# An fp32 two-layer hybrid trunk on one core: issuing the odd mixer's small steps by an estimate of the engines

## The chip, the core and the metric

The kernel runs on one core of one Trainium2 chip. Its engines are TensorE (PE; PEld is its weight load), VectorE (DVE), ScalarE (ACT), GpSimd (POOL) and SyncE (SP), which issues most DMAs. The metric is the device time of one launch in microseconds (us); lower is better. Times come from repeated runs; the profile is of one further execution.

## The reference

Sixteen meta tokens are put ahead of 256 frames of width 1024, T = 272 columns in all. Two layers follow, each `h += 1/2 SwiGLU(RMSNorm h); h += Mixer(RMSNorm h); h += 1/2 SwiGLU(RMSNorm h)`, in fp32, with a feed-forward width of 2816. The even mixer has a top-k sparse attention beside a chunkwise retention. The odd mixer, which the change is mostly about, is cut here to what matters:

```
cq, ck, cv, dx = split_cols(h @ w_in, [512, 128, 128, 512])
cq, ck = rms_norm(cq per head, c_qn), rms_norm(ck per head, c_kn)   # 8 query heads, 2 key heads of 64
yc = swa_sinks(cq, ck, cv, sinks)        # softmax over a window, the meta keys and one sink per head
yd = pool_mixer(dx, d_mix, d_scale)      # (mean over the last 2, 4, 8, 16 rows - x) @ mix, per group of 128
y  = concat(yc, yd) @ w_out              # 1024 x 1024
```

## The kernel before

**Layout.** The state h lies transposed, as eight tiles of 128 features x 272 columns. An fp32 product is made of three fast matmuls: operand and weight are each split into a rounded part (hi) and its remainder (lo), and `mmw` issues whi x xhi (L256), whi x xlo (L257), wlo x xhi (L258). One call is a block: one 128x128 weight tile against 256 or 272 columns. There are 2616 blocks in a fixed order, given by the `order_*` functions, and the weights lie packed in that order. Eight blocks make a unit (512 KB).

**Weights.** The class `Weights` loads chunks of one or two units over SP's queue into three buffers (`load`), and splits each unit: ACT rounds it to whi (L165), DVE subtracts to wlo (L166; POOL for a few units). Splits run four units ahead of PE; a ring holds six. In the mixers a unit is split in two halves, one at its first block and one in the middle (`halves`). At the start, h comes in four loads and the first weights in parts of 256 KB and whole units; the first 32 blocks go in rounds of one, one, two and four k over four groups (`order_ffn_in0`).

**The order of the small steps.** Everything but blocks is a generator (a task). Each block ends in `tick`, which moves a clock by one and resumes the tasks that are due; a task says by a number in the table `W` in how many ticks (blocks) it wants to go on. All engines take their instructions in this program order, so a step issued too early makes its engine wait with everything behind it. `drain` ticks until no task is left. `norm_r` (ones-matmul L311, table load, Ln, Exp, three DVE products) is issued at fixed blocks.

**The odd mixer** (`odd`). Ten groups of eight blocks (k = 0 to 7): keys, four pairs of query heads (256 columns), values, four pool groups; queries and pool groups alternate at the end. The first two groups leave out k = 7 until both are there (`_late_last_k`). A finished group is scaled by r into SBUF (`evac`, L435). Then `head_norm` (square on ACT L442, ones-matmul L446, `rsqrt` with Ln, Exp, one DVE product and POOL's L275 to L277, scale L450), `to_tokens` (transposes of the values, L459), or `pool_mix` (POOL sums L853, DVE L857, matmul L860, ACT L863, DVE L865). `attend` handles a pair of heads: scores L482, maxima on DVE L491, exponentials on ACT L498, normalisation L505, transposes ("turn", three PSUM banks) L513, copies L517 to L519, product with the values L528, outputs L530 and L532. One such attention is started every 8 ticks. The output has eight row tiles m of eight k: k = 7 to 4 (pools) and then k = 0 to 3 (attention) for the first four m, then the other four; `finish` adds a row tile to h, makes the next layer's xhi (L285) and xlo (L286), and POOL sums squares. PSUM has eight banks, one per accumulating group or small result.

Of the kernel before, what the change touches and what calls it, by code (L numbers as in the profile page):

```python
# [18 lines left out]
T = 272  # L19
# [40 lines left out]
def order_ffn_in0():  # L60

    g = [(p, j) for j in range(KF) for p in range(2)]
    return ([(x, k) for r in (range(1), range(1, 2), range(2, 4), range(4, 8)) for x in g[:4] for k in r]
            + [(x, k) for x in g[4:] for k in range(KD)])


def order_ffn_out():
# [7 lines left out]
OD_GROUPS = ([("ck", 0), ("cq", 0), ("cv", 0), ("cq", 1), ("dx", 3), ("cq", 2), ("dx", 2), ("cq", 3)]  # L75
             + [("dx", i) for i in (1, 0)])
# [16 lines left out]
def order_od_out():  # L93
    a, b = range(4), range(4, 8)
    return ([(m, k) for m in a for k in (7, 6, 5, 4)] + [(m, k) for m in a for k in range(4)]
            + [(m, k) for m in b for k in (4, 5, 6, 7, 0, 1, 2, 3)])
# [8 lines left out]
N_UNITS = sum(len(ORDERS[p[0]]()) for p in PHASES) // UNIT  # L105


def chunk_units():

    sizes, left = [1, 1, 1, 1], N_UNITS - 4  # L110
    while left:
        n = min(2, left)
        sizes.append(n)
        left -= n
    return sizes
# [3 lines left out]
W = dict(first_sq=2, hid=6, hid_lo=1, hn_sum=15, hn_out=15, od_hn=(4, 10), tok=15, tok_out=1,  # L119
         ev=dict(max=1, max2=2, exp=3, exp2=2, norm=2, norm2=2, turn=4, copy=2, pv=4, lo=1), ev_every=22,  # L120
         od=dict(max=1, max2=2, exp=2, exp2=2, norm=1, norm2=1, turn=3, copy=1, pv=3, lo=1), od_every=8,
         ix=10, ix_relu=1, ix_add=2, top_a=5, top_b=3, meta_k=8, meta=4, rope=10, rope_done=24, ret_every=10, ret_mask=1, ret_v=1, ret_s=2,
         ret_sum=7, ret_out=14, ret_lo=2, pool=3, pool_g=3, pool_mm=3, pool_lo=2)


class Weights:


    RAW, RING, AHEAD = 3, 6, 4

    def __init__(self, nc, pool, w):
        self.nc, self.pool, self.w = nc, pool, w
# [4 lines left out]
        self.halves, self.todo = False, None  # L137
        self.loaded = self.split_to = self.i = 0
# [12 lines left out]
    def load_part(self, i):  # L151

        n = UNIT * 128
        if i == 0:
            self.raw[0] = self.pool.tile([128, 2 * n], F32, tag="raw", name="raw", bufs=self.RAW)
        o = i * n // 2
        self.nc.sync.dma_start(self.raw[0][:, o:o + n // 2], bass.AP(
            tensor=self.w.tensor, offset=self.w.offset + o, ap=[[n, 128], [1, n // 2]]))
        self.loaded = 1

    def part(self, u, s):
# [4 lines left out]
        eng.tensor_tensor(lo[:, s], src[:, s], hi[:, s].bitcast(F32), op=OP.subtract)  # L166

    def split(self, upto, halves=False):
        while self.split_to < min(upto, N_UNITS):
            u, n = self.split_to, UNIT * 128  # L170
            c = self.chunk_of[u]
            self.load(c + 1)
            o = (u - self.first[c]) * n
            self.src[u] = self.raw[c][:, o:o + n]
            hi = self.pool.tile([128, n], F32R, tag="whi", name="whi", bufs=self.RING)
            lo = self.pool.tile([128, n], F32R, tag="wlo", name="wlo", bufs=self.RING)
            self.parts[u] = (hi, lo)
            self.parts.pop(u - self.RING, None)
            self.part(u, slice(0, n // 2) if halves else slice(0, n))
            if halves:  # L180
                self.todo = u
            self.split_to += 1
            if not halves:
                self.done_with(u)

    def second_half(self):
        if self.todo is not None:
            self.part(self.todo, slice(UNIT * 64, UNIT * 128))
            self.done_with(self.todo)
            self.todo = None  # L190
# [20 lines left out]
class Trunk:  # L211
    def __init__(self, tc, ctx, a, out):
        self.tc, self.nc, self.a, self.out = tc, tc.nc, a, out
# [4 lines left out]
        self.w = Weights(self.nc, self.ring, a["w"])  # L218
# [4 lines left out]
    def spawn(self, gen):  # L223
        self.tasks.append([self.clock, gen])

    def run_tasks(self):
        for t in list(self.tasks):
            while t[1] is not None and t[0] <= self.clock:
                try:
                    t[0] = self.clock + max(1, next(t[1]) or 1)  # L230
# [4 lines left out]
    def tick(self):  # L235
        self.clock += 1
        self.run_tasks()
# [12 lines left out]
    def bank(self, tag):  # L250
        return self.psum.tile([128, 512], F32, tag="bank", name=tag, bufs=8)

    def mmw(self, ps, hi, lo, start, stop):
        mm = self.nc.tensor.matmul
        wh, wl = self.w.next()
        mm(ps, wh, hi, start=start, stop=False)  # L256
        mm(ps, wh, lo, start=False, stop=False)  # L257
        mm(ps, wl, hi, start=False, stop=stop)  # L258
        self.tick()

    def rsqrt(self, out, mean, on=None):

# [6 lines left out]
        nc.scalar.activation(r0, r0, AF.Exp, scale=-0.5)  # L269
        nc.vector.scalar_tensor_tensor(u, mean, EPS, r0, op0=OP.add, op1=OP.mult)  # L270
# [8 lines left out]
    def prep_x(self, m, norm, c):  # L279

        nc = self.nc
        g = self.par[:, norm * KD + m:norm * KD + m + 1]
        hi = self.keep.tile([128, T], F32R, tag="xhi", name="xhi", bufs=KD)
        lo = self.keep.tile([128, T], F32R, tag="xlo", name="xlo", bufs=KD)
        nc.scalar.activation(hi[:, c], self.h[m][:, c], AF.Copy, scale=g)  # L285
        nc.vector.scalar_tensor_tensor(lo[:, c], self.h[m][:, c], g, hi[:, c].bitcast(F32),  # L286
                                       op0=OP.mult, op1=OP.subtract)
        self.x[m] = (hi, lo)

    def finish(self, m, ps, coef, norm, c):  # L290
# [11 lines left out]
        else:  # L302
            sq = self.keep.tile([128, T], F32, tag="sq", name="sq", bufs=2)
            nc.gpsimd.tensor_tensor(sq[:, c], h, h, op=OP.mult)  # L304
            nc.gpsimd.tensor_tensor(self.acc[:, c], self.acc[:, c], sq[:, c], op=OP.add)

    def norm_r(self, c):
# [7 lines left out]
        self.r = r  # L315


    def start(self):
        nc, a, keep = self.nc, self.a, self.keep
        hall = keep.tile([128, NPAR + KD * T], F32, name="h")  # L320
        self.par = hall[:, :NPAR]
# [13 lines left out]
        self.w.load_part(0)  # L335
        load_h(1, 2)
        self.w.load_part(1)
        load_h(2, 4)
        self.w.load(2)
        load_h(4, 8)  # L340
        self.w.load(Weights.RAW)
# [13 lines left out]
        self.x, self.acc, self.r = {}, None, None  # L355

    def first_x(self):

        nc, c = self.nc, slice(0, T)
        for m in range(KD):  # L360
            self.prep_x(m, 0, c)
            if m == 0:
                self.w.split(1, halves=True)
            elif m == 1:
                self.w.second_half()
            elif m == 3:
                self.w.split(2)

        def squares():
            yield W["first_sq"]  # L370
            for m in range(KD):
                sq = self.keep.tile([128, T], F32, tag="acc" if m == 0 else "sq", name="sq", bufs=2)
                nc.scalar.activation(sq, self.h[m], AF.Square)
                if m == 0:
                    self.acc = sq
                else:
                    nc.gpsimd.tensor_tensor(self.acc, self.acc, sq, op=OP.add)
                yield W["first_sq"]
        self.spawn(squares())

    def ffn(self, c, next_norm, first=False):
        nc = self.nc
        self.w.halves = False
        with ExitStack() as es:
# [3 lines left out]
            self.r = None  # L388
# [23 lines left out]
            for (p, j), k in (order_ffn_in0 if first else order_ffn_in)():  # L412
                if (p, j) not in banks:
                    banks[p, j] = self.bank("mm")[:, :n]
                hi, lo = self.x[k]
                d = done[p, j] = done.get((p, j), 0) + 1
                self.mmw(banks[p, j], hi[:, c], lo[:, c], d == 1, d == KD)
                if p == 1 and d == KD:
                    if j == (2 if first else 0):
                        self.norm_r(c)  # L420
                    self.spawn(act(j, banks.pop((0, j)), banks.pop((1, j))))
            for m, k in order_ffn_out():
# [10 lines left out]
    def evac(self, ps, pool, tag, bufs, c=slice(0, T)):  # L433
        t = pool.tile([128, T], F32, tag=tag, name=tag, bufs=bufs)
        self.nc.vector.tensor_tensor(t[:, c], ps, self.r[:, c], op=OP.mult)  # L435
        return t

    def head_norm(self, raw, gain, pool, put, c=slice(0, T), wt=None):

        nc = self.nc  # L440
        sq = pool.tile([128, T], F32, tag="hn_sq", name="hn_sq", bufs=2)[:, c]
        nc.scalar.activation(sq, raw[:, c], AF.Square)  # L442
        wt = wt or (W["hn_sum"], W["hn_out"])
        yield wt[0]
# [3 lines left out]
        self.rsqrt(rr, ps, nc.gpsimd)  # L448
        yield wt[1]
# [3 lines left out]
    def to_tokens(self, raw, put):  # L453

        nc = self.nc
        yield W["tok"]
# [3 lines left out]
        yield W["tok_out"]  # L460
        put(ps)

    def attend(self, pool, st, wt, i, qT, kT, v_cols, bias, yhi, ylo, sinks=None):
# [8 lines left out]
        e = int(sinks is not None)  # L472
        so = (0, NKEYS[0] + e)
# [560 lines left out]
```

## Time and profile before

| | us |
|---|---|
| median of the runs | 1092.91 (1092.13 to 1094.56) |
| the profiled execution | 1095.3 |
| its span, first to last instruction | 1093.5 |
| PE busy in it | 1077.0 |
| DVE busy | 713.5 |
| ACT busy | 521.1 |
| POOL busy | 178.9 |

A program shows what each engine did in the span. A busy PE is modelled from pipelined matmuls, whose durations overlap; the rate at which blocks start says more. "Idle before" a row is the time its engine stood still ahead of it, and the name behind the arrow is what ended that.

### The profile page before, as it was taken

What the parts mean: (1) busy time and instruction counts of PE and PEld (TensorE: products, weight loads), DVE (VectorE), ACT (ScalarE), POOL (GpSimd) and SP (SyncE); (2) the same over time, 40 slices, a digit from 0 to 9 for tenths busy, and PEclk for the clock granted to TensorE, in tenths of its full rate; (3) what the DMA queues carried; (4) which work ended last, traced back from release to release, by engine and by line L of the source; (5) the groups of instructions that cost most, each with busy time, mean ns of one, the idle gap of its engine ahead of it and who ended that gap; (6) DMA issues with size and microseconds to landing.
All of it is one profiled execution on the core that took longest, in us unless ns stands there. A gap on an engine that the chain in (4) does not pass through costs nothing.

```text
span 1093.5 us, 20686 instructions
## 1 busy us (share of the span) xinstructions
PE 1077.0 (98%) x8601; PEld 1056.8 (97%) x8601; DVE 713.5 (65%) x1217; ACT 521.1 (48%) x861; POOL 178.9 (16%) x223
## 2 busy tenths in 40 slices
PE   8999999999999999999999999999998899999998
PEld 7999999999899999999999999999997699999998
DVE  4776655399885677766655576665558767777642
ACT  6554443456545645544434454443436436554431
POOL 2000001448431741000002100000224221000000
PEclk9999999999999999999999999999999899999999
DMA  6554444543563334544554455454443224655551
GB/s 244 201 215 173 175 154 171 184 150 131 187 208 116 117 126 184 201 185 170 177 188 159 154 193 186 161 192 175 174 171 117 78 103 171 216 205 177 182 201 39
DMA packets 29805, 183.54 MB, mean 168 GB/s; under 512 B 3904, under 2 KB 6336, under 8 KB 8592
## 3 DMA queue, kind: packets, MB, share of 16 engines
q1 hardware_dynamic: 29440, 181.29, 45.9%
q8 instruction: 67, 1.10, 0.4%
q0 software_dynamic: 272, 0.94, 0.3%
q14 instruction: 26, 0.21, 0.1%
HBM read 180.02 MB, written 1.05 MB: 166 GB/s over the span
## 4 chain that ended last, share of the span: by engine, by line
PE 92%; DVE 3%; ACT 2%; DMA 1%; SPq 1%; issue 1%; POOL 0%; DVEq 0%; ACTq 0%
PE mm L256 29%; PE mm L257 29%; PE mm L258 29%; DMA raw<-in_w 1%; DVE wlo L166 1%; PE sd L513 1%; PE sd L528 1%; ACT whi L165 1%; PE sd L482 1%; PE sd L446 0%; SPq L630 0%; PE sd L703 0%; PE sd L729 0%; PE sd L737 0%; PE sd L599 0%
## 5 line engine op out<-in xcount | busy, mean ns | idle before, releaser
L256 PE MATMUL mm<-xhi,whi 128*128 128x272 f32 (+1 forms) x1816 | 532.8, 293 | 1.4 <-ACT whi L165 1.4
L258 PE MATMUL mm<-xhi,wlo 128*128 128x272 f32 (+1 forms) x1816 | 522.3, 288 | 1.0 <-DVE wlo L166 1.0
L257 PE MATMUL mm<-xlo,whi 128*128 128x272 f32 (+1 forms) x1816 | 521.9, 287 | 0.2
L166 DVE TENSOR_TENSOR wlo<-raw,whi 128x1024 fp32r<-128x1024 f32 (+1 forms) x394 | 414.9, 1088 | 81.0 <-ACT whi L165 80.0
L165 ACT ACTIVATE whi<-raw 128x1024 fp32r<-128x1024 f32 (+1 forms) x407 | 346.3, 895 | 30.5 <-PE mm L257 25.0
L256 PEld LDWEIGHTS mm<-xhi,whi 128*128 128x128 f32 x1816 | 344.0, 189 | 8.1 <-issue 4.5
L258 PEld LDWEIGHTS mm<-xhi,wlo 128*128 128x128 f32 x1816 | 344.5, 190 | 1.5 <-DVE wlo L166 1.5
L257 PEld LDWEIGHTS mm<-xlo,whi 128*128 128x128 f32 x1816 | 343.5, 189 | 1.5 <-DVE xlo L286 0.6
L258 PE MATMUL mm<-hhi,wlo 128*128 128x272 f32 (+1 forms) x704 | 201.4, 286 | 0.0
L257 PE MATMUL mm<-hlo,whi 128*128 128x272 f32 (+1 forms) x704 | 201.4, 286 | 0.0
L256 PE MATMUL mm<-hhi,whi 128*128 128x272 f32 (+1 forms) x704 | 201.1, 286 | 0.0
L256 PEld LDWEIGHTS mm<-hhi,whi 128*128 128x128 f32 x704 | 132.6, 188 | 0.0
L257 PEld LDWEIGHTS mm<-hlo,whi 128*128 128x128 f32 x704 | 132.5, 188 | 0.0
L258 PEld LDWEIGHTS mm<-hhi,wlo 128*128 128x128 f32 x704 | 132.5, 188 | 0.0
L399 ACT ACTIVATE gr<-gr 128x272 f32<-128x272 f32 (+1 forms) x88 | 37.7, 428 | 153.8 <-DVE gr L397 153.8
L285 ACT ACTIVATE xhi<-h 128x272 fp32r<-128x272 f32 (+1 forms) x48 | 24.6, 520 | 154.3 <-DVE h L294 150.7
L294 DVE SCALAR_TENSOR_TENSOR h<-mm,h 128x272 f32<-128x272 f32 (+1 forms) x48 | 20.8, 433 | 115.7 <-PE mm L258 115.7
L404 ACT ACTIVATE hhi<-ur 128x272 fp32r<-128x272 f32 (+1 forms) x88 | 37.6, 428 | 91.0 <-DVE ur L401 91.0
L301 POOL TENSOR_TENSOR acc<-h 128x272 f32<-128x272 f32 (+1 forms) x5 | 3.2, 634 | 431.5 <-DVE h L294 431.5
L398 DVE TENSOR_TENSOR ur<-mm,r 128x272 f32<-128x272 f32 (+1 forms) x88 | 38.2, 434 | 43.9 <-PE mm L258 43.8
L407 DVE TENSOR_TENSOR hlo<-ur,hhi 128x272 fp32r<-128x272 f32 (+1 forms) x88 | 38.5, 438 | 41.9 <-ACT hhi L404 41.9
L304 POOL TENSOR_TENSOR sq<-h 128x272 f32<-128x272 f32 (+1 forms) x35 | 22.2, 634 | 157.8 <-DVE h L294 157.8
(161 smaller groups left out, 867.0 us busy)
## 6 DMA issues: line engine op xcount, KB each, us to landing
raw<-in_w SPq DMA_DIRECT2D x165, 1024.0 KB, 4.8
tab<-in_tab SPq DMA_DIRECT2D x8, 272.0 KB, 5.0
raw<-in_w SPq DMA_DIRECT2D x4, 512.0 KB, 6.2
sw<-ev_t SPq DMA_DIRECT2D x32, 34.0 KB, 3.3
out<-h SPq DMA_DIRECT2D x8, 128.0 KB, 1.7
h<-in_h SPq DMA_DIRECT2D x1, 544.0 KB, 7.3
raw<-in_w SPq DMA_DIRECT2D x2, 256.0 KB, 3.5
h<-in_h SPq DMA_DIRECT2D x1, 272.0 KB, 5.7
```

Source lines behind the costliest of these rows:

```text
L165: self.nc.scalar.activation(hi[:, s], src[:, s], AF.Copy)
L166: eng.tensor_tensor(lo[:, s], src[:, s], hi[:, s].bitcast(F32), op=OP.subtract)
L256: mm(ps, wh, hi, start=start, stop=False)
L257: mm(ps, wh, lo, start=False, stop=False)
L258: mm(ps, wl, hi, start=False, stop=stop)
L285: nc.scalar.activation(hi[:, c], self.h[m][:, c], AF.Copy, scale=g)
L294: nc.vector.scalar_tensor_tensor(h, ps, coef, h, op0=OP.mult, op1=OP.add)
L304: nc.gpsimd.tensor_tensor(sq[:, c], h, h, op=OP.mult)
L398: nc.vector.tensor_tensor(ur[:, c], pu, r, op=OP.mult)
L399: nc.scalar.activation(gr[:, c], gr[:, c], AF.Silu)
L404: nc.scalar.activation(hi[:, c], ur[:, c], AF.Copy)
L407: nc.vector.tensor_tensor(lo[:, c], ur[:, c], hi[:, c].bitcast(F32), op=OP.subtract)
```

## The change

- The start: h is loaded tile by tile, the weights of the first 32 blocks four blocks at a time beside it, and those blocks run k by k over four groups. All chunks have two units.
- `_late_last_k` holds back the last two k of the first two groups in place of the last one.
- A class `Plan` keeps an estimate of when each engine is free and each tensor ready, fed by wrappers around the engines. In the odd mixer a task waits, in place of a number of ticks, for `after(engine, operands)`: until the operands are estimated ready at that engine's time or PE's. `room(k)` makes it wait until k of the eight banks are free beside a reserve. Evacuations are tasks too. A wlo subtraction is held until its whi is estimated ready, or its unit is wanted.
- The odd mixer's groups go keys, first queries, values, the other queries, then the pool groups. At most two attentions are in flight. The sinks are copied by POOL. The head norms' rsqrt ends on DVE. The output runs k = 7 to 4 over all eight m, two m to a bank, then k = 0 to 3 by m; `finish2` handles two row tiles together, with the squares on ACT, and its last ones run on into the next layer.
- From 110 blocks before the odd mixer the splits run further ahead, by up to eight halves; after the even mixer the ring has ten units.
- `norm_soon` issues a norm when its sum is estimated ready. The three pauses of the even mixer's meta attention are 8 ticks in place of 4.

The core of the diff:

```diff
-    out = [(g, k) for g in groups[:late] for k in range(kn - 1)]
-    out += [(g, kn - 1) for g in groups[:late]]
+    out = [(g, k) for g in groups[:late] for k in range(kn - 2)]
+    out += [(g, k) for k in (kn - 2, kn - 1) for g in groups[:late]]
...
+    return [(x, k) for k in range(KD) for x in g[:4]] + [(x, k) for x in g[4:] for k in range(KD)]
...
-OD_GROUPS = ([("ck", 0), ("cq", 0), ("cv", 0), ("cq", 1), ("dx", 3), ("cq", 2), ("dx", 2), ("cq", 3)]
-             + [("dx", i) for i in (1, 0)])
+OD_GROUPS = ([("ck", 0), ("cq", 0), ("cv", 0), ("cq", 1), ("cq", 2), ("cq", 3)] + [("dx", i) for i in (3, 2, 1, 0)])
...
+    return ([(m, k) for k in (7, 6, 5, 4) for m in range(KD)] + [(m, k) for m in range(KD) for k in range(4)])
...
+MORE_AHEAD = ([OD_AT + b for b in (-110, -8, 16, 108, 112, 144)], (0, 8, 8, 3, 3, 0))
...
+    def ready(self, eng, aps, slack=0.0):
+        t = max((self.at.get(a.name, 0.0) for a in aps), default=0.0)
+        return t <= max(self.free["PE"], self.free[eng]) + slack
...
+                busy, mode = (0.5 if half else 1.0) * 1.67 * n, self.HALF if half else self.FULL
+            if mode != self.mode:
+                busy, self.mode = busy + 200, mode
+            late = 150
+        elif eng == "DVE":
+            busy, late = 95 + 1.03 * n, 120
+            if op == "tensor_tensor_reduce":
+                busy += 80
+            if self.free["POOL"] > self.free["DVE"]:
+                busy *= 1.25
+        elif eng == "ACT":
+            busy, late = 100 + 0.84 * n, 150
...
+    def low(self, upto=None):
+
+        while self.lows and (self.plan.ready("DVE", [self.lows[0][2]]) if upto is None and self.wait
+                             else upto is None or self.lows[0][0] <= upto):
...
-        if j == 0:
-            self.split(u + self.AHEAD, self.halves)
-        elif j == UNIT // 2:
-            self.second_half()
+        if j in (0, UNIT // 2):
+            extra = int(np.interp(self.i, *MORE_AHEAD))
+            self.split(2 * (u + self.AHEAD) + extra - (self.halves and j == 0))
+        self.low(u)
...
+    def room(self, k):
+
+        while self.live + k + self.reserve > 8:
+            yield 1
...
+        nc.vector.tensor_tensor(h, two(ps), h, op=OP.add)
+        yield self.after("ACT", h)
+        for m in ms:
+            self.x_hi(m, norm, c)
+        sq = [self.keep.tile([128, T], F32, tag="sq", name="sq", bufs=2) for _ in ms]
+        for m in ms:
+            nc.scalar.activation(sq[m - ms[0]][:, c], self.h[m][:, c], AF.Square)
+        yield self.after("DVE", self.xh[ms[1]])
+        for m in ms:
+            self.x_lo(m, norm, c)
...
+    def norm_soon(self, c):
+
+        self.r = None
+        while self.summed < KD:
+            yield 1
+        yield self.after("PE", self.acc)
+        self.norm_r(c)
...
+        self.w.load_part(0, 2)
+        self.w.load_part(2, 2)
+        for m in range(1, KD):
+            load_h(m, m + 1)
+            self.w.load_part(4 * m, 4)
+        for i in (32, 40):
+            self.w.load_part(i, 8)
...
+            yield self.after("ACT", ps)
+            yield from self.rsqrt_steps(rr, ps)
+            self.live -= 1
+            yield self.after("DVE", rr)
...
-                    while i not in got["cq"] or not got["ck"] or not st["vC"]:
+                    while i not in got["cq"] or not got["ck"] or not st["vC"] or st.get("turned", 0) < i - 1:
...
+            self.live, self.reserve, self.w.wait = 0, 2, True
+            self.spawn(self.norm_soon(c))
+            self.spawn(attention())
...
+                    if g == OD_GROUPS[-1]:
+                        self.reserve = 4
...
+                self.mmw(banks[b][:, half * SEQ:half * SEQ + SEQ], hi[:, cx], lo[:, cx], d == 1, d > 14, True)
+                if d == 16:
+                    self.spawn(self.finish2(b, banks.pop(b), next_norm))
+                    self.run_tasks()
```

## Rows read from the trace of the kernel before

**Rows 1.** The page's busy times of the engines over the span.
```profile
PE 1077.0 (98%) x8601; PEld 1056.8 (97%) x8601; DVE 713.5 (65%) x1217; ACT 521.1 (48%) x861; POOL 178.9 (16%) x223
```

**Rows 2.** Busy time by stretch: stretch, length, engines (instructions), granted clock, DMA share, GB/s.
```profile
30.00:100.00 70.00, 70.00 (x558) 70.00 (x556) 52.43 (x84) 37.00 (x55) 0.00 (x0) 1.00 0.53 194
...
760.00:819.00 59.00, 59.00 (x474) 59.00 (x473) 30.71 (x39) 22.85 (x29) 12.10 (x16) 1.00 0.49 183
819.00:845.00 26.00, 22.05 (x169) 20.21 (x169) 19.95 (x52) 14.23 (x36) 10.47 (x13) 1.00 0.37 131
845.00:885.00 40.00, 35.70 (x274) 30.98 (x273) 25.34 (x76) 18.91 (x53) 9.00 (x12) 0.87 0.16 55
...
960.00:1025.00 65.00, 65.00 (x549) 65.00 (x548) 45.42 (x71) 32.49 (x48) 0.00 (x0) 1.00 0.53 193
```

**Rows 3.** PE's waits: line, what it waited for, us in total, times, longest.
```profile
PE sd L446 <- ACT hn_sq L442: 3.4, 2, 1.8
PE sd L513 <- DVE at_s L505: 2.5, 3, 1.9
...
PE mm L256 <- ACT oyhi L863: 1.1, 2, 0.6
PE sd L648 <- DVE ms L645: 1.0, 1, 1.0
...
PE sd L860 <- DVE at_m L502: 0.8, 1, 0.8
```

**Rows 4.** PE's timeline at the start: first matmuls of blocks 5, 11, 16, 33.
```profile
7.00 0.39 PE L256 MATMUL mm<-xhi,whi 128*128 128x272 f32 x1
...
12.53 0.36 PE L256 MATMUL mm<-xhi,whi 128*128 128x272 f32 x1
...
15.87 0.36 PE L256 MATMUL mm<-xhi,whi 128*128 128x272 f32 x1
...
22.36 0.29 PE L256 MATMUL mm<-xhi,whi 128*128 128x272 f32 x1
```

**Rows 5.** DMA from 0 to 40 us: GB/s per us; one load, KB, us to landing.
```profile
GB/s 0 35 319 201 209 293 317 385 423 418 406 250 74 176 401 393 221 401 442 393 401 229 41 8 25 8 115 344 418 311 385 426 98 66 287 410 303 0 0 0
...
h<-in_h SPq DMA_DIRECT2D x1, 168.0 KB, 2.3
```

**Rows 6.** PE's timeline: first block of the odd mixer, first of the last layer.
```profile
814.38 0.29 PE L256 MATMUL mm<-xhi,whi 128*128 128x272 f32 x1
...
900.62 0.28 PE L256 MATMUL mm<-xhi,whi 128*128 128x256 f32 x1
```

**Rows 7.** The chain that ended last, pieces in the odd mixer: start, us, what.
```profile
842.87 0.43 PE sd L446 x2
843.67 1.09 PE sd L513 x10
...
846.66 1.25 PE sd L528 x20
...
851.94 0.90 PE sd L482 x8
```

**Rows 8.** Timelines of POOL and DVE: end of a head norm's rsqrt; a DVE product.
```profile
826.26 1.32 POOL L275 TENSOR_TENSOR rs<-rs,rs 128x272 f32<-128x272 f32 x1 [8.37 <-DVE rs L270]
...
828.17 1.09 POOL L277 TENSOR_TENSOR hn_r<-rs,rs 128x272 f32<-128x272 f32 x1
...
822.01 0.44 DVE L272 SCALAR_TENSOR_TENSOR rs<-rs,rs 128x272 f32<-128x272 f32 x1
```

**Rows 9.** Timelines of PE and ACT: a small matmul and its reader.
```profile
833.13 0.70 PE L446 MATMUL sd<-hn_sq,ones_h 128*128 128x256 f32 x2 [1.76 <-ACT hn_sq L442]
...
833.93 0.48 ACT L268 ACTIVATE rs<-sd,eps 128x256 f32<-128x256 f32 x1 [0.33 <-PE sd L446]
```

**Rows 10.** PE's timeline at the start of the last layer.
```profile
902.88 0.38 PE L256 MATMUL mm<-xhi,whi 128*128 128x256 f32 x1
903.40 0.39 PE L257 MATMUL mm<-xlo,whi 128*128 128x256 f32 x1
```

More of the change, by code (lines that the diff above doesn't have):

```diff
@@ new lines, with __init__, __getattr__, call @@
+class Engine:
+    def __init__(self, real, plan, name):
+        self.real, self.plan, self.name = real, plan, name
+    def __getattr__(self, op):
+        f = getattr(self.real, op)
+        def call(*a, **k):
+            r = f(*a, **k)
+            self.plan.note(self.name, op, a, k)
+            return r
+        return call
+class Engines:
+    def __init__(self, nc, plan):
+        self.nc, self.sync = nc, nc.sync
+        self.tensor, self.vector, self.scalar, self.gpsimd = (
+            Engine(e, plan, n) for e, n in ((nc.tensor, "PE"), (nc.vector, "DVE"), (nc.scalar, "ACT"),
+                                            (nc.gpsimd, "POOL")))
+    def get_next_instruction_name(self):
+        return self.nc.get_next_instruction_name()
@@ L165, in part @@
         self.nc.scalar.activation(hi[:, s], src[:, s], AF.Copy)
[L166 to L183, printed above, removed]
-                self.done_with(u)
@@ new lines, in lengthen, with open_unit @@
+    def lengthen(self, pool):
+        self.pool2 = pool
+    def open_unit(self, u):
+        n = UNIT * 128
+        c = self.chunk_of[u]
+        self.load(c + 1)
+        o = (u - self.first[c]) * n
+        self.src[u] = self.raw[c][:, o:o + n]
+        pool, name, bufs = self.pool, "", self.RING
+        if self.pool2:
+            if self.at >= self.RING:
+                pool, name, bufs = self.pool2, "2", self.MORE
+            self.at = (self.at + 1) % (self.RING + self.MORE)
+        self.parts[u] = tuple(pool.tile([128, n], F32R, tag=t + name, name=t + name, bufs=bufs) for t in ("whi", "wlo"))
+        self.parts.pop(u - self.RING - self.MORE, None)
@@ L192, in done_with, with split @@
+    def split(self, goal):
+        while self.split_to < min(goal, 2 * N_UNITS):
+            u, half = divmod(self.split_to, 2)
+            if not half:
+                self.open_unit(u)
+            n = min(2 - half, goal - self.split_to)
+            self.split_to += n
+            self.pending[u] = self.pending.get(u, 2 if not half and n == 1 else 1)
+            self.part(u, slice(half * UNIT * 64, (half + n) * UNIT * 64))
     def done_with(self, u):
@@ L223, in spawn, with after @@
     def spawn(self, gen):
-        self.tasks.append([self.clock, gen])
+        self.tasks.append([self.clock, gen, None])
+    def after(self, eng, *aps):
+        return lambda: self.plan.ready(eng, aps)
+    def room(self, k):
+        while self.live + k + self.reserve > 8:
+            yield 1
     def run_tasks(self):
+        if self.w.wait:
+            self.w.low()
         for t in list(self.tasks):
-            while t[1] is not None and t[0] <= self.clock:
+            while t[1] is not None and t[0] <= self.clock and (t[2] is None or t[2]()):
                 try:
-                    t[0] = self.clock + max(1, next(t[1]) or 1)
+                    v = next(t[1])
+                    t[2] = v if callable(v) else None
+                    if t[2] is None:
+                        t[0] = self.clock + max(1, v or 1)
                 except StopIteration:
@@ L233, in run_tasks, with tick @@
                     self.tasks.remove(t)
-    def tick(self):
+    def tick(self, idle=True):
         self.clock += 1
+        if idle:
+            self.plan.free["PE"] += 125
         self.run_tasks()
@@ L250, in bank, with mmw, rsqrt_steps @@
     def bank(self, tag):
+        self.live += 1
         return self.psum.tile([128, 512], F32, tag="bank", name=tag, bufs=8)
-    def mmw(self, ps, hi, lo, start, stop):
-        mm = self.nc.tensor.matmul
+    def mmw(self, ps, hi, lo, start, stop, shared=False):
+        mm = self.nc.nc.tensor.matmul
         wh, wl = self.w.next()
[L256 to L259, printed above, removed]
+        mm(ps, wh, hi, start=start, stop=False, skip_group_check=shared)
+        mm(ps, wh, lo, start=False, stop=False, skip_group_check=shared)
+        mm(ps, wl, hi, start=False, stop=stop, skip_group_check=shared)
+        if self.plan.mode != Plan.FULL:
+            self.plan.mode = Plan.FULL
+            self.plan.free["PE"] += 200
+        self.plan.put("PE", [ps], [wh, wl, hi, lo], 3 * (4 + 0.445 * ps.shape[-1]), 150)
+        self.tick(idle=False)
     def rsqrt(self, out, mean, on=None):
+        for _ in self.rsqrt_steps(out, mean, on):
+            pass
+    def rsqrt_steps(self, out, mean, on=None):
         nc = self.nc
@@ L387, in ffn @@
                 self.first_x()
-            self.r = None
+            if not first:
+                self.spawn(self.norm_soon(c))
             hid, banks, turn = {}, {}, [0]
@@ L414, in ffn @@
                     banks[p, j] = self.bank("mm")[:, :n]
+                while k not in self.x:
+                    self.tick()
                 hi, lo = self.x[k]
@@ L472, in attend, with step @@
         e = int(sinks is not None)
+        def step(name, eng, *aps):
+            return wt[name] if wt else self.after(eng, *aps)
         so = (0, NKEYS[0] + e)
@@ L476, in attend @@
         mn, tot, inv = (sm[:, 4 * a:4 * a + 4] for a in range(3))
+        if e:
+            nc.gpsimd.tensor_copy(s[:, :, NKEYS[0]::T + 1], sinks.unsqueeze(2).to_broadcast([128, 2, 2]))
+        if not wt:
+            yield self.after("PE", qT, kT)
+            yield from self.room(2)
         pss = [self.bank("sd"), self.bank("sd")]
@@ L498, in attend @@
                 nc.scalar.activation(v, v, AF.Exp, bias=mn[:, a:a + 1], scale=-1.0, accum_out=tot[:, a:a + 1])
-            yield wt["norm" if t else "exp2"]
+            yield step("norm" if t else "exp2", "DVE" if t else "ACT", *([s] if t else []))
         for t in range(2):
@@ L505, in attend @@
                 nc.vector.tensor_scalar(v, v, inv[:, a:a + 1], None, op0=OP.mult)
-            yield wt["turn" if t else "norm2"]
+            yield step("turn" if t else "norm2", "PE" if t else "DVE", *([s] if t else []))
+        if not wt:
+            yield from self.room(3)
         turned = [self.bank("sd") for _ in range(3)]
@@ L519, in attend @@
         nc.scalar.copy(pt[2], turned[2][:, :256])
-        yield wt["pv"]
+        self.live -= 3
+        yield step("pv", "PE", *pt)
+        if not wt:
+            yield from self.room(1)
         ps = self.bank("sd")[:, :SEQ]
@@ L529, in attend @@
                                      start=(kt == 0), stop=(kt == 1 + t))
+        if not wt:
+            yield self.after("ACT", ps)
         nc.scalar.activation(yhi[:, META:T], ps, AF.Copy)
-        yield wt["lo"]
+        yield step("lo", "DVE", yhi)
         nc.vector.tensor_tensor(ylo[:, META:T], ps, yhi[:, META:T].bitcast(F32), op=OP.subtract)
+        self.live -= 1
         st["att"] += 1
@@ L755, in even @@
                     banks[g] = self.bank("mm")[:, :cc.stop - cc.start]
+                while k not in self.x:
+                    self.tick()
                 hi, lo = self.x[k]
@@ L873, in odd @@
                 if g not in banks:
-                    banks[g] = self.bank("mm")[:, :cc.stop - cc.start]
+                    if g == OD_GROUPS[-1]:
+                        self.reserve = 4
+                    banks[g] = bank()[:, :cc.stop - cc.start]
+                while k not in self.x:
+                    self.tick()
                 hi, lo = self.x[k]
```

288 lines of the change are left out of this document (183 added, 105 removed).

## The prediction

> **What bounds the kernel now.** I read the page's busy times first: PE is busy for 1077.0 of 1093.5 us [rows 1], so only what makes PE wait, run slower or do less can move the end. The stretches come next [rows 2]. From 30 to 100 us, 558 matmuls take 70.00 us, 0.1254 us each, at a full clock. One block (a 128x128 weight tile, three matmuls) is thus 0.376 us at 272 columns; from 960 to 1025, 549 in 65.00 us give 0.355 us at 256. The feed-forward layers run at this rate without idle time. Two stretches don't: 819 to 845 has PE busy for 22.05 of 26 us, and 845 to 885 for 35.70 of 40, there with the clock at 0.87. That is the odd mixer. PE's waits name the same place [rows 3]: L446, L513, L256 on oyhi and L860 add up to 7.8 us, all of them small steps of the odd mixer that stand in PE's queue before their operand is there. One more wait lies in the even mixer (L648, 1.0 us). The third place is the start: block 5 begins at 7.00 us, block 33 at 22.36 [rows 4], so 28 blocks took 15.4 us where 28 x 0.376 = 10.5 would do.
>
> The profiled execution took 1095.3 us, 1.8 more than its span and 2.4 more than the median of the runs, 1092.91. I subtract the same sum from both.
>
> **The change part by part.**
>
> *Start.* Blocks 1 to 32 now run k by k (four blocks per k), and their loads come as one h tile and four blocks (136 + 256 KB, 0.40 MB) per k; 17 loads stand where nine stood. The bytes ahead of block 5 are the same, so it starts at about 7.0 again. From there a step is PE's 4 x 0.376 = 1.50 us, or the loading of 0.40 MB. While small pieces arrived (slices 4 to 6) the queue moved 201 to 293 GB/s, mean 234; behind them 317 to 423 [rows 5], so 1.71 down to about 1.0 us a step. I take the middle, so PE sets the pace: block 33 at 7.0 + 10.5 = 17.5, a gain of 4.9. At 234 GB/s block 29 comes at 7.0 + 6 x 1.71 = 17.3 and block 33 at 18.8: gain 3.6. Before, blocks 11 to 15 took 3.34 us (12.53 to 15.87) [rows 4], 1.5 more than 5 x 0.376: PE ran at the lower clock behind a pause. Were that to return on top, the gain is 2.1. I take **4.0**, bounds 2.1 and 4.9. SP's queue has the weights of block 48 and on behind eight more issues, due only after 22 us: nothing. ACT does the squares between the splits, 0.5 + 0.5 + 0.5 us per step against 1.5: it just fits, and is covered by the lower bound.
>
> The Trainium skill, page "DMA: Bandwidth & Descriptors", section "Anatomy of one DMA", fits a transfer issued by GpSimd as about 2.0 us fixed plus its bytes. By that rule eight more loads in series would put the start back by 16 us instead of winning 4; the smallest load here, 168 KB, took 2.3 us [rows 5], which agrees with the fixed part and leaves open whether loads overlap (rival 3).
>
> *Even mixer.* The three pauses of the meta attention go from 4 to 8 ticks, that is 4 x 0.376 = 1.5 us later each. The stall of 1.0 us at L648 [rows 3] goes; what is later next, three short steps, is not wanted before attention ends much later. **1.0**, bounds 0 and 1.0.
>
> *Odd mixer, the work.* It runs from 814.38 to 900.62 [rows 6]: 86.2 us. Big blocks: 48 x 0.376 + 96 x 0.355 = 52.1. Small steps, by the pieces of the chain [rows 7]: four attentions x (0.90 + 1.09 + 1.25) = 13.0; five head norms and, of the same shape, four pools x 0.43 = 3.9; the norm and the value transposes, put at the same 0.43, 0.9. Together 17.8, so 69.9 us of PE work and 16.3 us of loss: 7.8 of named waits, the rest a lower clock (0.87 over 40 us) and refilling PE after a small step. Neither count changes: PE does the same blocks and the same 4 x 3 + 5 + 4 + 2 = 23 small steps.
>
> *Odd mixer, what moves.* (a) A small step is issued only when an estimate has its operand ready, and a block goes in instead. (b) Queries go first, and 32 output blocks (k = 7 to 4 over all eight m, before: 16 over four) stand ready to fill: 32 x 0.355 = 11.4 us. (c) The head norm's last products leave POOL, where L275 to L277 ran from 826.26 to 829.26, 3.0 us, for two DVE instructions of 0.44 [rows 8]: every head is ready 2.1 us earlier. (d) Half-unit splits run eight halves ahead, so a wlo that waits behind attention on DVE starves no matmul. Price of (c) and (d): 5 x 2 x 0.44 = 4.4 us more on DVE, less five halves of about 0.7 us pushed out of the stage. DVE was busy 19.95 + 25.34 of 66 us [rows 2] and stays near 46 of at least 62: cover enough. The four units ahead cost ACT and DVE some 4 x 1.2 us each before the stage, where DVE is busy 30.71 of 59 us and the DMA engines 0.49 [rows 2]: nothing; without that cover 4.8.
>
> What remains of the 16.3? The estimate puts a 256-column small matmul at 1.67 ns x 256 + 150 = 577 ns to its reader. The trace has L446 start at 833.13 and ACT start on it at 833.93, 0.80 us [rows 9]. So the estimate runs early by up to 0.22 a step; I take 0.15 of waiting and 0.07 of refilling for each of 23 steps: 5.0 us stay, **11.3** are gained. Bounds: 0.35 a step (8.1 stay), gain 8.2; nothing stays but refill (1.6), gain 14.7. Keeping the full clock is part of this gain.
>
> *Into the last layer.* Before, PE waited there for xlo: 902.88 to 903.40 where 0.12 is normal [rows 10], 0.4 us, and the norm's start and refills cost a little beside it, 0.6 as an estimate. The rows of h now come in pairs: one add, two copies, two squares, two subtractions; five of these before x[7], at about 0.5 us [rows 8] 2.5 us, against 12 blocks x 0.355 = 4.3 us that now need neither x[6] nor x[7]. **0.5**, bounds -0.5 (five steps at 1.0 us, where splits stand between) and 0.6. Norms issued earlier elsewhere: nothing, PE waits for none there.
>
> Sum: 4.0 + 1.0 + 11.3 + 0.5 = 16.8. The profiled execution would take 1078.5, the median **1076.1 us**. By the bounds the gain is 9.8 to 21.2.
>
> **Rivals.**
>
> 1. *Half the stalls stay.* Eight PSUM banks are shared: a turn of attention needs three free ones with two to four held back, so attentions may queue for banks and end late, and PE waits for oyhi as it did at L256 [rows 3]. For it: reserve 4 as the last group starts. Against: 11.4 us of filler. Half of 11.3 stays and the start gives its lower bound: gain 5.6 + 2.1 + 1.0 = 8.7, **1084.2**. Chance 0.13.
>
> 2. *Estimates that run early* (the other side). PE takes its queue in order, so each of the 23 steps that is issued too early stops all blocks behind it. The two waits at L446 were 1.7 us each [rows 3]. If every step waited so long, 23 x (1.7 - 0.15) = 35.7 us would be added: **1111.8**. It decides once the mean wait passes 0.15 + 16.8 / 23 = 0.88 us. Against: such waits were five or six of 23 before, and the new estimates are near the rows. Chance 0.06.
>
> 3. *Loads in series.* A load of 168 KB took 2.3 us to land, of which some 0.4 are bytes at 400 GB/s [rows 5]: 1.9 us. Eight more of them one after the other: 15 us, the start loses 11 instead of gaining 4: **1091.1**, no change. Against: several loads were in flight while 423 GB/s moved. Chance 0.04.
>
> 4. *Low clock from many small waits.* The clock fell behind the waits of 845 to 885 (0.87), but held 1.00 from 819 to 845 with waits too [rows 2, 3]. Were half of the 69.9 us run at the lower of the two levels, 1.2 for 2.4 GHz, 35 us would be added: **1111**; it decides from 17 us of such work. Chance 0.03. The Trainium skill, page "TensorE: Matmul & The Clock Gate", section "A second HAM failure mode: psum-queue depth-cycling", tells of a kernel in which frequent short idle gaps between matmul groups made the clock oscillate; here it has worked for one stretch and not for the other.
>
> 5. *The plan changes no order that matters*: the odd stage stays at 86 us, gain 5.5, **1087.4**. Chance 0.04.
>
> **How the numbers follow.** Forecast 0.70, rivals 0.13, 0.06, 0.04, 0.03, 0.04. Time: the forecast's 1076.1. Range: its bounds give 1071.7 to 1083.1; to take in most of rival 1 I go to **1085**, and **1071.5** below. A measurement tells 0.2%, about 2.2 us, from no change: faster 0.70 + 0.13 + 0.04 = 0.87, same 0.04, slower 0.06 + 0.03 = 0.09.
>
> **What would show it.** Block 33 at 17 to 19 us; no wait at L648's matmul; the odd mixer, first xhi block to the first of the last layer, 72 to 78 us, its clock 1.00 throughout, its PE waits under 4 us in sum; DVE under 50 us in it; no wait for x[6] or x[7]. Wrong: PE waits over 0.5 us each at head norms or turns (rival 2), a wait for oyhi (rival 1), block 5 later than 8 us (rival 3), a clock under 0.9 (rival 4).

## The result and the profile after

The changed kernel takes 1078.2 us (median of 4 runs, 1077.91 to 1078.53) against 1092.52 us for the kernel before: a ratio of 0.9867, 95% interval 0.985 to 0.9884. It is faster by 14.3 us, where 16.8 were forecast (1076.1, range 1071.5 to 1085). The profiled execution took 1078.34 us, its span 1076.6.

The page's busy times and its row of the granted clock over 40 slices come first (answer to [rows 1]):

```profile
PE 1069.2 (99%) x8601; PEld 1051.6 (98%) x8601; DVE 718.0 (67%) x1223; ACT 522.3 (49%) x877; POOL 164.5 (15%) x204
...
PEclk9999999999999999999999999999999999999999
```

PE has the same number of instructions; three in each of 2680 blocks are block matmuls (2680 by the order functions and the trace, not the 2616 of the description). Its wall time is shorter by 16.9 us, of which its busy time fell by 7.8 and its idle time by 9.1: part of the "busy" time before was work at a lower clock.

The odd mixer as one stretch shows it, in the kernel before and then in the changed one (columns as in [rows 2]):

```profile
814.38:900.62 86.24, 77.99 (x609) 71.44 (x608) 60.79 (x153) 44.66 (x108) 30.08 (x40) 0.94 0.28 96
```

```profile
812.24:883.68 71.44, 71.36 (x609) 67.44 (x608) 55.20 (x146) 42.32 (x108) 15.49 (x22) 1.00 0.29 107
...
829.00:869.00 40.00, 39.92 (x350) 36.59 (x349) 36.45 (x107) 25.57 (x73) 9.79 (x12) 1.00 0.26 92
```

The same 609 matmul records take 71.44 us in place of 86.24. PE stands still for 8.25 us before and for 0.08 after; the clock goes from 0.94 to 1.00. DVE is busy 36.45 of the 40 us from 829 to 869, and PE does not feel it. PE's waits over the whole span (answer to [rows 3]; the helper L199 now records every small step):

```profile
PE sd L199 <- DVE eps L199: 1.2, 1, 1.2
PE mm L392 <- ACT whi L199: 1.1, 1, 1.1
PE mm L394 <- DVE wlo L199: 0.8, 3, 0.3
PE sd L199 <- DVE at_s L199: 0.3, 1, 0.3
PE mm L393 <- DVE xlo L199: 0.2, 1, 0.2
```

Nothing of the odd mixer is left in this list. The row on eps belongs to the warm-up matmuls ahead of the first block, at_s to the even mixer, xlo to the last layer. The whi and wlo rows belong to the start; there PE's timeline has blocks 5 and 33 at (answer to [rows 4]):

```profile
7.98 0.40 PE L392 MATMUL mm<-xhi,whi 128*128 128x272 f32 x1 [1.06 <-ACT whi L199]
...
20.30 0.29 PE L392 MATMUL mm<-xhi,whi 128*128 128x272 f32 x1
```

Block 5 is later than before (7.00), block 33 earlier (22.36), by 2.1 us where 4.0 were forecast. DVE's timeline, and POOL's behind it, tell of a cause in between:

```profile
3.60 0.50 DVE L199 SCALAR_TENSOR_TENSOR xlo<-h,xhi 128x272 fp32r<-128x272 f32 x1 [2.46 <-ACT xhi L199]
...
10.92 0.68 DVE L199 TENSOR_TENSOR wlo<-raw,whi 128x512 fp32r<-128x512 f32 x1
11.52 1.01 DVE L199 SCALAR_TENSOR_TENSOR xlo<-h,xhi 128x272 fp32r<-128x272 f32 x1
```

```profile
11.05 2.12 POOL L199 TENSOR_TENSOR sq<-sq 128x272 f32<-128x272 f32 x2 [0.36 <-ACT sq L199]
```

The same subtraction took 0.50 us at 3.60, before POOL had anything to add; at 11.52 POOL adds squares, and it takes 1.01. The run with the squares behind the loop (below) separates the two: there POOL is still until 16.49, and all eight of these subtractions take 0.49 to 0.50. The Trainium skill, page "GPSIMD Engine Reference", section "8. Key points", says that GpSimd shares its SBUF interfaces with VectorE and contends with instructions that read two SBUF inputs, as this one does; the trace agrees, with 1.01 for 0.50.

### The profile page after: what moved, and what is told of

Read it like the earlier page. It is cut to its first block, busy times and chain, and to the rows that moved or that the text cites. A ratio compares the mean times of both kernels' runs of the same rounds, so it can differ in the third digit from the quotient of the medians.

```text
span 1076.6 us, 20688 instructions
## 1 busy us (share of the span) xinstructions
PE 1069.2 (99%) x8601; PEld 1051.6 (98%) x8601; DVE 718.0 (67%) x1223; ACT 522.3 (49%) x877; POOL 164.5 (15%) x204
## 4 chain that ended last, share of the span: by engine, by line
PE 96%; DVE 2%; ACT 1%; DMA 0%; issue 0%; SPq 0%; DVEq 0%; ACTq 0%
PE mm L392 30%; PE mm L394 30%; PE mm L393 30%; PE sd L199 6%; DVE wlo L199 1%; DMA raw<-in_w 0%; ACT whi L199 0%; DVE xlo L199 0%; DVE h L199 0%; ACT xhi L199 0%; ACT sq L199 0%; SPq L248 0%; SPq L515 0%; ACT at_s L199 0%; DVE at_s L199 0%
## 5 line engine op out<-in xcount | busy, mean ns | idle before, releaser
L199 DVE TENSOR_TENSOR wlo<-raw,whi 128x1024 fp32r<-128x1024 f32 (+2 forms) x402 | 415.1, 1069 | 73.0 <-ACT whi L199 72.3
L199 ACT ACTIVATE whi<-raw 128x1024 fp32r<-128x1024 f32 (+2 forms) x415 | 345.7, 881 | 31.2 <-DMA raw<-in_w 31.1
L199 ACT ACTIVATE gr<-gr 128x272 f32<-128x272 f32 (+1 forms) x88 | 37.7, 428 | 155.1 <-DVE gr L199 152.9
L199 ACT ACTIVATE xhi<-h 128x272 fp32r<-128x272 f32 (+1 forms) x48 | 24.5, 518 | 145.2 <-DVE h L199 144.2
L199 DVE SCALAR_TENSOR_TENSOR h<-mm,h 128x272 f32<-128x272 f32 (+1 forms) x40 | 17.5, 437 | 109.4 <-PE mm L394 109.4
L199 ACT ACTIVATE hhi<-ur 128x272 fp32r<-128x272 f32 (+1 forms) x88 | 37.7, 428 | 97.7 <-DVE ur L199 97.7
L199 DVE TENSOR_TENSOR ur<-mm,r 128x272 f32<-128x272 f32 (+1 forms) x88 | 38.3, 435 | 50.3 <-PE mm L394 50.3
L199 POOL TENSOR_TENSOR acc<-h 128x272 f32<-128x272 f32 x4 | 2.6, 640 | 419.7 <-DVE h L199 419.7
L199 DVE TENSOR_TENSOR hlo<-ur,hhi 128x272 fp32r<-128x272 f32 (+1 forms) x88 | 38.5, 438 | 42.0 <-ACT hhi L199 42.0
L199 DVE TENSOR_TENSOR ur<-gr,ur 128x272 f32<-128x272 f32 (+1 forms) x88 | 38.6, 438 | 13.1 <-ACT gr L199 5.5
```

The source lines that it names most:

```text
L199: r = f(*a, **k)
```

## The experiments

Each kernel is the changed one with a single edit, unless its text says otherwise. Lengths of the odd mixer run from its first xhi block to the first of the last layer, as in [rows 6].

The changed kernel was not run again beside the experiments, and in their rounds the medians of the kernel before differ by 2.3 us (1091.13 to 1093.46). What a part is worth is therefore read from the length of its stage. In the six profiles that leave the odd mixer as changed it took 71.42 to 71.44 us, so a few tenths count there. The start is less steady: in the eight profiles with the changed start block 33 began between 19.75 and 20.93.

**The kernel before, again.** No edit.

> The kernel before once more, for a second profile. The first profile of it lay 2.4 us above the median of its runs. Theory A: the odd mixer's length varies from run to run with the clock that falls behind its waits, so this profile has block 33 at about 22.4 us again and an odd mixer shorter than 86.2 us by as much as its time is nearer to the median (about 84 us at 1092.5). Rival B: the start varies (its own stretch of low clock, 1.5 us), block 33 then comes at about 20.9 us and the odd mixer stays at 86.2 us.

It took 1092.81 us, 2.5 less than its first profile. Block 33 came at 21.82 (0.5 earlier), the even mixer gave 0.4, and the odd mixer, in the same view as above, was 84.76 long:

```profile
813.39:898.15 84.76, 76.47 (x609) 70.19 (x608) 60.83 (x153) 44.65 (x108) 30.09 (x40) 0.96 0.28 98
```

The idle time is the same (8.29); 1.5 us less went into work at the lower clock. So A, though the start and the even mixer had a part too. Over all its runs the kernel before spread from 1089.42 to 1094.65, the changed one, in four runs only, from 1077.91 to 1078.53.

**The start undone.**

```diff
-    return [(x, k) for k in range(KD) for x in g[:4]] + [(x, k) for x in g[4:] for k in range(KD)]
+    return ([(x, k) for r in (range(1), range(1, 2), range(2, 4), range(4, 8)) for x in g[:4] for k in r]
+            + [(x, k) for x in g[4:] for k in range(KD)])
...
+        self.w.load_part(0, 4)
+        load_h(1, 2)
+        self.w.load_part(4, 4)
+        load_h(2, 4)
+        self.w.load_part(8, 8)
+        load_h(4, 8)
```

(The squares are a task again, the splits follow the loads.)

> The changed kernel with the start of before: its loads, its rounds of one, one, two and four k, its splits and its squares as a task. By the two profiles block 33 came 2.1 us earlier in the changed kernel, so theory A: 2.1 us slower than the changed kernel, 1080.3. Rival B (the start of before is slow only in some runs, where its clock falls): under 0.8 us slower, below 1079.0.

1079.11 us, 0.9 above the changed kernel: between the two, nearer to B. Block 33 came at 20.90, not at 22.36: this execution had no stretch of lower clock (1.000 over its span). That is still within the 19.75 to 20.93 of the changed start, so by this block alone the run shows no gain of the start clear of its variation.

**Squares behind the loop.**

```diff
-            if m:
-                square(m - 1)
-        square(KD - 1)
+        for m in range(KD):
+            square(m)
```

> The changed kernel with the eight squares and POOL's sums behind the loop over k, where they don't run beside DVE's splits. In the changed kernel DVE's xlo took 1.00 us beside POOL and 0.50 without it, and PE lost 1.1 us at blocks 17 and 29 for a late wlo. Theory A: these two go, block 33 at 19.2, 1077.1. Rival B (the loads' arrival sets the pace): nothing changes, 1078.2.

1082.74 us, 4.5 slower: neither. The wait at block 17 went (blocks 17 to 28 took 4.55 us for 5.13) and block 29 did come 0.6 earlier (17.60). But the eight squares stood in ACT's queue ahead of the next unit's split, five of them waiting 0.4 to 0.6 us each for POOL's sums, and PE waited for that split. Its longest wait from 15 to 30 us:

```profile
PE mm L392 <- ACT whi L199: 2.8, 1, 2.8
```

**One first load.**

```diff
-        self.w.load_part(0, 2)
-        self.w.load_part(2, 2)
+        self.w.load_part(0, 4)
-            for i, n in ((0, 2), (2, 2)) if m == 0 else ((4 * m, 4),):
+            for i, n in ((4 * m, 4),):
```

> The changed kernel with the first four blocks as one load of 256 KB, as before the change, in place of two of 128 KB; all else as changed. Theory A: the extra issue and the small rows put the second k's weights back (split at 7.30 against 6.31 before), so block 5 comes at about 7.1 in place of 7.98 and 0.8 us are won less 0.1 at block 1, 1077.5. Rival B (the single h tiles and four-block loads behind them share the queue and set it): block 5 stays at about 8.0, 1078.2 to 1078.4.

1077.97 us (1077.82 to 1078.13), no different from 1078.2. Block 1 came 0.7 later, block 5 at 7.85: nearer to B. What sets block 5's arrival was not found; it lay between 7.00 and 8.18 in the profiles.

**Both, with the squares as a task.** One load as above, and:

```diff
-            if m:
-                square(m - 1)
-        square(KD - 1)
+        def squares():
+            yield 12
+            for m in range(KD):
+                square(m)
+                yield 3
+        self.spawn(squares())
```

> The changed kernel with the start's squares as a task behind the loop over k (one from the twelfth block on, then one every third block, between the splits of the next units), and the first four blocks as one load. Theory A (POOL's sums beside DVE's splits cost PE the two late wlo, and ACT's queue has room between the next units): block 33 at 19.0 to 19.3, 1 us less than the changed kernel, 1077.1. Rival B (the squares stop ACT's splits again, as when they stood in one row): block 33 at 20 or later, 1078.2 or more.

1080.6 us (1079.08 to 1081.45), 2.4 slower. The time is B's, but not for B's reason: block 33 came at 19.14 as in A, and then POOL's sum was late and PE stood at the first norm. PE's wait from 20 to 40 us, and the stretch around it with its clock of 0.93:

```profile
PE sd L199 <- POOL sq L199: 2.3, 1, 2.3
```

```profile
20.00:30.00 10.00, 7.74 (x55) 7.45 (x55) 6.10 (x5) 7.67 (x13) 7.19 (x7) 0.93 0.67 229
```

In the changed kernel the squares between the splits cost two late wlo, and pay for it with a norm that is ready in time. No version here beat the changed kernel by more than the spread of its runs.

**The estimate off.**

```diff
-        return t <= max(self.free["PE"], self.free[eng]) + slack
+        return True
```

> The changed kernel with the estimate switched off: ready() says yes always, so each task goes on one block after its last step, as soon as banks allow. Order of groups, filler and banks stay. Theory A (the estimate wins the odd mixer's 14.8 us by keeping PE, DVE and ACT from standing behind a step issued too early): 23 small steps on PE wait about 1 us each, 1078.2 + 23 = 1101, at least 1090. Rival B (the new order and the 32 filler blocks win it, whenever steps are issued): below 1082.

1145.67 us, a ratio of 1.0482 (1.0461 to 1.0503) to the kernel before: A, and nearly three times its price. The edit goes further than was expected of it: a step that is always ready follows the last one in the same tick, with no block between them, where the kernel before left one block or more. PE's timeline has one attention like this, without a block from the first row to the last:

```profile
844.90 0.60 PE L199 MATMUL sd<-ident,at_s 128*72 128x128 f32 x4 [2.09 <-DVE at_s L199]
845.97 0.87 PE L199 MATMUL sd<-ident,at_s 128*72 128x128 f32 x6 [0.47 <-DVE at_s L199]
846.77 2.40 PE L199 MATMUL sd<-at_p,vC 72*64 72x128 f32 x20
```

So the run prices steps issued at once; it does not price the old ticks. The odd mixer took 123.83 us, 52.4 more. Some of PE's waits over the span, and the stage:

```profile
PE sd L199 <- POOL acc L199: 14.6, 5, 6.3
PE sd L199 <- DVE at_s L199: 9.5, 7, 2.1
PE sd L199 <- DVE py L199: 7.7, 4, 2.6
```

```profile
821.84:945.67 123.83, 94.83 (x609) 84.60 (x608) 56.95 (x144) 41.67 (x103) 12.48 (x21) 0.79 0.17 62
```

PE stands still for 29 us of it, and its busy time is 94.83 for 71.36, at a granted clock of 0.79 among the waits. The rest of the loss lies mostly at the norms (acc), which are now issued before their sum is there.

**Every step 300 ns early.**

```diff
-    def ready(self, eng, aps, slack=0.0):
+    def ready(self, eng, aps, slack=300.0):
```

> The changed kernel with every step allowed 300 ns before its estimated time. Theory A (what was predicted: the estimate has no margin on PE, so each of 23 steps would wait 0.3 us more): 7 us, 1085. Rival B (PE runs behind the estimate, by refills and what else the estimate leaves out, so that steps come with room): under 2 us lost, 1078.2 to 1080.

1079.47 us, 1.3 slower; the odd mixer 73.04, 1.6 longer: B. Of 6.9 us in steps most found room.

**The rsqrt's end on POOL.**

```diff
-            yield from self.rsqrt_steps(rr, ps)
+            self.rsqrt(rr, ps, nc.gpsimd)
```

> The changed kernel with the odd head norms' rsqrt ended by POOL's three instructions as before, issued at once and not step by step. Theory A (attention has time to spare: its last product with the values ran at 861.4, and the blocks that need it began near 868.5): heads come 2 to 3 us later and nothing is lost, 1078.2 to 1079. Rival B (the chain of the heads bounds the stage): five norms of 2.1 us, two or more of them on the chain, 1082 or more.

1080.1 us, 1.9 slower, the odd mixer 73.38, 1.9 longer: between the two. PE waited for the heads at two scores:

```profile
PE sd L199 <- DVE od_t L199: 1.4, 2, 0.9
```

**Half the filler.**

```diff
-    return ([(m, k) for k in (7, 6, 5, 4) for m in range(KD)] + [(m, k) for m in range(KD) for k in range(4)])
+    a, b = range(4), range(4, 8)
+    return ([(m, k) for k in (7, 6, 5, 4) for m in a] + [(m, k) for m in a for k in range(4)]
+            + [(m, k) for k in (7, 6, 5, 4) for m in b] + [(m, k) for m in b for k in range(4)])
```

> The changed kernel with the output blocks in two halves of four row tiles, so that 16 blocks of the pools stand ahead of the first that needs attention, as before, in place of 32. Theory A (attention ends some 6 us before the end of 32 filler blocks, 16 of them are 5.7 us): at most 1 us is lost, 1078.2 to 1079.2. Rival B (the filler is what hides attention): the wait for oyhi is back, 3 us or more, 1081 and over.

1079.87 us (1078.56 to 1081.08); the odd mixer 72.70, 1.3 longer, with the wait for attention back, once:

```profile
PE mm L394 <- ACT oyhi L201: 0.9, 1, 0.9
```

Between the two, nearer to A.

**The groups as before.**

```diff
-OD_GROUPS = ([("ck", 0), ("cq", 0), ("cv", 0), ("cq", 1), ("cq", 2), ("cq", 3)] + [("dx", i) for i in (3, 2, 1, 0)])
+OD_GROUPS = ([("ck", 0), ("cq", 0), ("cv", 0), ("cq", 1), ("dx", 3), ("cq", 2), ("dx", 2), ("cq", 3)]
+             + [("dx", i) for i in (1, 0)])
```

> The changed kernel with the groups in the order of before, two pool groups between the queries, so that the last queries come 16 blocks (6 us) later. Theory A: the last attention ends up to 6 us later, at about the end of the filler; 0 to 2 us are lost, 1078.2 to 1080. Rival B (queries first is what shortens the stage): 4 to 6 us are lost, 1082 to 1084.

1078.28 us; the odd mixer 71.86, 0.4 longer: A. Queries first are worth next to nothing with the rest in place.

**Half the splits ahead.**

```diff
-MORE_AHEAD = ([OD_AT + b for b in (-110, -8, 16, 108, 112, 144)], (0, 8, 8, 3, 3, 0))
+MORE_AHEAD = ([OD_AT + b for b in (-110, -8, 16, 108, 112, 144)], (0, 4, 4, 2, 2, 0))
```

> The changed kernel with half the splits ahead: up to four halves, two from block 108 of the odd mixer. Theory A (DVE is busy 36 of the 40 us from 829 to 869 in the changed kernel, so the splits done before the stage are what keeps a wlo from being late): waits of PE for wlo in the odd mixer, 1 to 4 us lost, 1079.5 to 1082. Rival B (four units ahead would do as before the change): nothing lost, 1078.2 to 1078.8.

1078.02 us, the odd mixer 71.32: B. No wait for a wlo in it. None ahead at all was not tried.

**Meta attention's pauses at 4.**

```diff
-         ix=10, ix_relu=1, ix_add=2, top_a=5, top_b=3, meta_k=8, meta=8, rope=10, rope_done=24, ret_every=10, ret_mask=1, ret_v=1, ret_s=2,
+         ix=10, ix_relu=1, ix_add=2, top_a=5, top_b=3, meta_k=8, meta=4, rope=10, rope_done=24, ret_every=10, ret_mask=1, ret_v=1, ret_s=2,
```

> The changed kernel with the pauses of the even mixer's meta attention at 4 ticks again. Theory A (the prediction's term): the wait of 1.0 us at the transpose of the meta attention is back and the time is 1.0 us longer, 1079.2. Rival B (the stall is refilled elsewhere in the even mixer, whose length from block 33 to the odd mixer was the same in both profiles within 0.1 us): the wait is back, the time stays within 0.4 us, 1077.8 to 1078.6.

1079.0 us, 0.8 slower, and the wait is back:

```profile
PE sd L199 <- DVE ms L199: 1.5, 1, 1.5
```

Nearer to A: block 33 to the odd mixer took 792.67 us against 791.94.

## Why the prediction held, and where it was off

**The place and the mechanism** were right. The odd mixer lost its waits and its lower clock, and 14.8 of the 16.9 us between the two profiles lie there. The start gave 2.1 and the even mixer 0.8. The two feed-forward layers between the mixers, as one stretch, gave 0.7 back, and the last layer with the tail came out even. That the new order needs its steps held back is shown: issued at once, the same order of blocks takes 52.4 us more in this stage. That the estimate does this better than the old ticks would, in the new order and with the larger filler, is argued and not shown: this middle way was not tried. For it speaks that undoing the groups, the filler or the rsqrt, one at a time, gave back 1.9 us at most.

**The sum** agrees better than its terms. Between the two profiles 16.9 us were won, for 16.8 forecast; but the odd mixer gave 3.5 more than its term and the start 1.9 less, the even mixer 0.2 and the last layer 0.5 less, and 0.7 were lost where nothing was booked. That these cancel is luck. Of the signs named, the clock, the sum of PE's waits and the one at L648's place held. Block 33 (20.30, not 17 to 19), the odd mixer (71.44, not 72 to 78), DVE's busy time and a small wait for xlo did not.

**"I subtract the same sum from both"** failed. The profiled execution of before stood 2.4 us above its median mostly because more of the odd mixer ran at the low clock, 1.5 us more than in the second profile, with 0.5 at the start and 0.4 in the even mixer beside it: largely the very loss that the change takes away. Against the second profile (1092.81) the change wins 14.5: 13.3 in the odd mixer, 1.5 at the start, 0.3 in the even one, less the 0.7. That is near the 14.3 of the medians.

**"5.0 us stay"** was too much. I booked 0.15 us of waiting and 0.07 of refilling on each of 23 steps. The stage took 71.44 us against the 69.9 of work that I had counted, so 1.5 stay, 0.07 a step, which is what I had put for refilling alone; the 14.8 gained lie just past the bound of 14.7. PE's idle time in it is 0.08 us. The early reader of [rows 9] is ACT: ACT waits for such a sum three times in the stage, 2.9 us in all, and PE does not. I put the wait on PE. That PE has room is shown by the 300 ns experiment, why it has it is not.

**"So PE sets the pace"** (start, 4.0) failed. Block 5 did not begin at 7.0 but at 7.98; its weights, which the text had called the same bytes, were there for ACT's split at 7.30 and not at 6.31. That is 1.0. Block 5 then lost 0.6 more at its own wlo. Two further wlo came late beside POOL's sums, about 1.1; the text costed the squares on ACT and left out their sums on POOL. Of PE's 4.9 this leaves the 2.1 of the profiles. It equals the lower bound by chance, since that was put on a clock that would fall again, and the clock stayed at 1.00. By the undone start, which had no low clock at all, the gain is 0.9.

**Even mixer** (1.0): 0.8 by the first profile, 0.7 by the experiment, 0.3 by the second profile of before.

**Into the last layer** (0.5): 0.3 from its first block to its late ones, and a wait for xlo of 0.23 us is left there at 888.46; the tail took 0.3 more. DVE was forecast under 50 us in the stage and has 55.20; that bound came from 66 us of it [rows 2], while all of it had 60.79 before.

**The rivals.** 1, half the stalls: not here; with half the filler one wait of 0.9 came back. 2, estimates that run early: its price is real, 52.4 us in the stage for steps issued at once, 2.3 a step and not 1.6: 29 us of it are waits, 1.3 a step, and the rest is work at the lower clock. 3, loads in series: block 33 came earlier, not later. Its price read 168 KB as the smallest load of before, at 2.3 us; one of 136 KB took 4.0. 4, the clock: 1.00 here, but 0.79 with the estimate off, among waits of up to 3.4 us. The Trainium skill, page "TensorE: Matmul & The Clock Gate", section "A second HAM failure mode: psum-queue depth-cycling", tells of a kernel whose clock oscillated because its matmul groups had frequent short gaps between them. The trace with the estimate off agrees, with a granted clock of 1.00 from 840 to 846 us, 0.50 from 847 to 853 and 1.00 from 885 to 890; the changed kernel has no such gaps in this stage. Rival 5, no change in this stage, is out: 71.44 for 86.24.

**Parts in the changed kernel,** each undone by itself: estimate 52.4, rsqrt on DVE 1.9, filler 1.3, order of groups 0.4, splits ahead (half) none, in us of the stage. They don't add up. A likely reason, not shown, is that the estimate puts a block wherever a step isn't ready and so hides most of what the others would save.

## What to carry to other kernels

Where one engine bounds and takes its queue in order, issue each small step when its operands are there, and keep independent blocks ready to stand in: here PE's idle time in the stage went from 8.25 to 0.08 us, and with both in place the order of the groups was worth only 0.4. Whether well chosen counts would do as well was not tried. Price a lower clock as part of the waits that bring it, and before adding a saving to a median, ask whether the profile's distance from that median is the same loss. When work moves to a helper, ask what the engine beside it pays: POOL's sums doubled DVE's subtraction at the start, 0.50 to 1.01 us.

## What the runs showed of the hardware

The time of the kernel before varied by 5 us from run to run, that of the changed one by 0.6 over its four runs. In the two profiles of the kernel before, the idle time of the odd mixer was the same within 0.04 us, and the clock 0.94 and 0.96: the same waits did not cost the same clock each time. One thing stays open: the first 320 blocks behind the even mixer took 15.13 us per 40 in the changed kernel and 15.07 in the kernel before, 0.7 us in all (121.65 against 121.00). Most variants have the longer time; four have the shorter one: the estimate off (behind its first 40 blocks), the 300 ns, the old groups, the rsqrt on POOL. No wait shows there.
